# A trunk's mixer: PE's order left to the scheduler, or written out in groups of attention steps and projection chunks

## The chip, the cores and the metric

The kernel runs on one core of one Trainium2 chip. The metric is the device time of one execution in microseconds (us). The core has a matrix engine (TensorE, PE in the profile, with its weight loads as PEld), a vector engine (VectorE, DVE), a scalar engine (ScalarE, ACT), GpSimd (POOL) and SyncE (SP), which here only issues DMAs. Each engine runs its own queue of instructions in a fixed order and waits for the others through semaphores.

## The reference

Two layers over 256 tokens of width 1024. Each layer is a mixer and then a mixture of experts, each with a residual and a layer norm behind it. The mixer multiplies the tokens by one wide input projection and splits its columns among three causal token mixers and three gates:

```
nq, kc, vc, ks, vs, kw, vw, ng, dq, dk, dv, cq, ckv, kr, mg = split_cols(h @ w_in, IN_SPLITS)
o_nsa = nsa_mixer(...)      # 8 heads: compressed, selected and window attention, gated
o_diff = diff_mixer(...)    # 4 heads: softmax(q1 k1) - lam * softmax(q2 k2), then rms norm
o_mla = mla_mixer(...)      # 8 heads: latent attention, up-projections of cq and ckv, rope
g = sigmoid(mg).reshape(B, S, 3, D_MODEL)
y = g[:, :, 0] * (o_nsa @ w_br_nsa) + g[:, :, 1] * (o_diff @ w_br_diff) + g[:, :, 2] * (o_mla @ w_br_mla)
return y @ w_out
```

The experts are 16 SwiGLU networks with a routing that keeps two experts per token. Weights and data are float32.

## The kernel before

**Projections in chunks.** Every projection is cut into chunks that stand in a list `fq`. `F(n)` (L394) takes `n` of them. A chunk first splits its weights into a high and a low half (`split`, L365: a cast on ScalarE, L369, and a subtraction on VectorE, L370; two pairs of buffers), one chunk ahead of its use, then runs three matmuls per piece of 128 rows (`mm3`, L373, the lines L374 to L376), then empties its accumulator (`pa`, two PSUM buffers). `add_fm` (L408) makes feature-major chunks: 24 matmuls of 256 columns for q, kv, dq, dk and the gates, twelve for a branch projection. `add_tm` (L437) makes token-major ones, which fill both accumulators. Weights come through a ring of buffers on SP's queue (`Stream`, L80); a buffer is given back by `ST.done`, and `ST.add(ring, ...)` hands further buffers to the experts' weights once the attention no longer holds them.

**Attention in steps.** `cmp1` to `cmp6` (L505 to L613) build the compressed keys and values and their softmax. `cmp1` swaps the two groups' halves with small matmuls (L513); `cmp2(k0)` (L524) runs eight matmuls of one weight buffer (L533, 32 columns of weights each), and its last call also turns the hidden layer and starts its activation. `nsa_A(n)` (L667) computes the scores of two heads (`scores`, L629, matmuls at L624, one PSUM pair of buffers), their row maxima on VectorE (L639, L641) and the exponentials on ScalarE (`expo`, L646); `nsa_B(n)` (L678) scales them (L650) and transposes them (`transp`, L654, L627, two PSUM buffers `pT`, copied out by VectorE at L658); `nsa_C(i)` (L691) multiplies with the values. `diff_A` to `diff_D` (L729 to L770) and `mla_Z`, `mla_A`, `mla_B`, `mla_C` (L841 to L874) do the same for the other two mixers; `mla_Z` makes the transposed queries and keys of two heads through two `pT` buffers (copied at L849), `mla_n` and `mla_t` (L796, L806) normalise the latents and turn them, `mla_up` (L820) queues their up-projections, `mla_rope` (L833) is VectorE alone.

**Order.** The source writes attention steps and chunks in turn: `go(...)` (L1023) runs one step, then one chunk. But this order is only a priority. The program is built with `schedule_with_timeline_sim=True` (L1784): the framework lays the instructions of each engine in an order of its own, taking what its estimate says is ready; only data dependences and edges made by `tc.issue_after(ins)` bind it. Such an edge keeps the instructions traced in its block, on the engine of `ins`, behind `ins` in issue order, with no wait for `ins` to finish. Within a step, `row` (L615) chains matmuls so. Between steps and chunks nothing is chained.

Of the kernel before, what the change touches and what calls it, by code (L numbers as in the profile page):

```python
# [68 lines left out]
def trunk(ctx, tc, x, consts, pcol, rowv, gb, wfm, wng, wdv, wmla, wcmp, wcmp2, wu, wbr, wout, rw, mw1, mw3, mw2, out):  # L69
    import numpy as np  # L70
    nc = tc.nc
    slopes = [float(v) for v in _slopes(np)]
    V, A, T, G = nc.vector, nc.scalar, nc.tensor, nc.gpsimd

    cst = ctx.enter_context(tc.tile_pool(name="cst", bufs=1))
    hp = ctx.enter_context(tc.tile_pool(name="hp", bufs=1))
# [265 lines left out]
    def mixer(l, res, z, zf):  # L342
# [35 lines left out]
        fq = []  # L378
# [15 lines left out]
        def F(n=1):  # L394
            for _ in range(n):
                if not fq:
                    return
                c = fq.pop(0)
                c.ready()
                for d in fq:  # L400
                    d.ready()
                    if d.grp is None or d.grp != c.grp:
                        break
                for _ in c.mm(c.h):
                    pass
                c.post()
# [95 lines left out]
        X = {}  # L502
        xT = []

        def cmp1():  # L505
            cx, kvc = X["cx"], X["kvc"]
            XS = cx.tile([P, 2, 16, 2, 16], F32, name="XS", tag="x5")
            V.memset(XS[:, :, :, :, 15:16], 0.0)
            sw = pT.tile([P, 2, P], F32, name="pt")
            rows = [slice(64 * g, 64 * g + 64) for g in range(2)]  # L510
            for i in range(2):
                for g in range(2):
                    T.matmul(sw[rows[1 - g], i], ident[rows[g], rows[g]], kvc[rows[g], i, 1 - g], start=True, stop=True)  # L513
            for i in range(2):
                p0 = PC_POS + 32 * l + 16 * i
                for g in range(2):
                    for a in (g, 1 - g):
                        base = kvc[rows[a], i, a] if a == g else sw[rows[a], i]
                        src = bass.AP(tensor=base.tensor, offset=base.offset, ap=[list(base.ap[0]), [1, 16], [8, 15]])
                        V.tensor_tensor(out=XS[rows[a], i, :, g, 0:15], in0=src, op=ALU.add,  # L520
                                                           in1=pc[rows[a], p0:p0 + 16].unsqueeze(2).to_broadcast([64, 16, 15]))
            X["XS"] = XS

        def cmp2(k0):  # L524
            XS = X["XS"]
            if k0 == 0:
                X["hid"] = pO.tile([P, 256], F32, name="o")
            X["wc"] = ST.get((l, "c", k0 // 4)).rearrange("p (i k c) -> p i k c", i=2, k=4)
            hid, wc = X["hid"], X["wc"]
            for k in range(k0, k0 + 4):  # L530
                for i in range(2):
                    o = 64 * (k % 2) + 32 * i
                    T.matmul(hid[o:o + 32], XS[:, i, k].rearrange("p g c -> p (g c)"), wc[:, i, k % 4],  # L533
                             start=(k < 2), stop=(k > 13), skip_group_check=True)
            ST.done((l, "c", k0 // 4))
            if k0 < 12:
                return
            cx = X["cx"]
            hs = X["t1"][:, 512:768]
            A.copy(hs, hid)  # L540
            hid = pO.tile([64, 256], F32, name="o")
            T.matmul(hid, id2, hs, start=True, stop=True)
            hx = cx.tile([64, 3, 256], F32, name="hx", tag="x6")
            A.copy(hx[:, 0], hid)
            V.tensor_mul(hx[:, 1], hx[:, 0], hx[:, 0])
            V.tensor_scalar(hx[:, 1], hx[:, 1], 0.044715, 1.0, op0=ALU.mult, op1=ALU.add)
            V.tensor_mul(hx[:, 1], hx[:, 1], hx[:, 0])
            A.activation(hx[:, 2], hx[:, 1], AF.Tanh, scale=math.sqrt(2.0 / math.pi))
            V.tensor_scalar(hx[:, 2], hx[:, 2], 1.0, 0.5, op0=ALU.add, op1=ALU.mult)
            V.tensor_mul(hx[:, 2], hx[:, 2], hx[:, 0])  # L550
            X["hx"] = hx
# [54 lines left out]
        def cmp6():  # L606
            cp = X["cp"]
            cpp = pT.tile([P, 2, S], F32, name="pt")
            for t in range(2):
                for hf in range(2):  # L610
                    T.transpose(cpp[:, hf, t * P:(t + 1) * P],
                                cp[:, t, 4 * hf:4 * hf + 4].rearrange("p a c -> p (a c)"), ident)
            A.copy(cpT, cpp)  # L613
# [264 lines left out]
        def gates(b, j):  # L878
            def ev(m, ps):
                if j == 0 and m == 0:  # L880
                    gate[b] = (mh if b % 2 else mg).tile([P, KD, S], F32, name="gt", tag=f"gt{b % 2}")
                A.activation(gate[b][:, 4 * j + m], ps, AF.Tanh, scale=0.5)
            add_fm(f"g{b}{j}", xT, 4, ev)
# [63 lines left out]
        with tc.issue_after(X0["z", 1 if "yh" in X0 else 3]):  # L947
            i = A.copy(gl[:, 0], w[:, 0:4])
# [57 lines left out]
        cx = X["cx"] = M["ml"] = left.enter_context(tc.tile_pool(name="cx", bufs=1, reuse_waits="tile"))  # L1006
# [7 lines left out]
        G.tensor_add(id2, ident[:, 0:64], ident[:, 64:P])  # L1014
        kvc = X["kvc"] = X["t1"][:, 0:512].rearrange("p (i a j) -> p i a j", i=2, a=2)

        F(8)
        V.tensor_scalar(gts, gts, 1.0, 0.5, op0=ALU.add, op1=ALU.mult)
        add_fm("dq", xT, 4, lambda m, ps: A.copy(dqT[:, m], ps))
        add_fm("dk", xT, 4, lambda m, ps: A.copy(dkT[:, m], ps))  # L1020
        add_tm("dv", xT, 512, lambda t, ps: A.copy(dv[:, t], ps))

        def go(*items):  # L1023
            for it in items:
                it()
                F()

        def z(f, *a):
            return lambda: f(*a)

        cmp1()
        diff_prep()
        go(z(nsa_A, 0), z(cmp2, 0), z(nsa_A, 1), z(cmp2, 4), z(nsa_B, 0), z(cmp2, 8), z(nsa_B, 1), z(cmp2, 12))
        go(z(nsa_A, 2), cmp3, z(nsa_A, 3), cmp4)
        cmp5()
        F(2)
        cmp6()
        if l == 0:
            router_prep()
        mla_in()  # L1040
        gates(0, 0)
        gates(0, 1)
        go(z(nsa_C, 0), z(nsa_B, 2), z(nsa_A, 4), z(nsa_B, 3), z(nsa_A, 5), z(nsa_C, 1), z(nsa_B, 4), z(nsa_A, 6), z(nsa_B, 5),
           z(nsa_A, 7), z(nsa_C, 2), z(nsa_B, 6), mla_n, z(nsa_B, 7), z(diff_A, 0), z(nsa_C, 3), mla_t)
        ST.add(ring, [f"wt{NA}"])
        ST.pump()
        F(2)
        mla_up(0)
        gates(1, 0)
        branch(0)  # L1050
        gates(1, 1)
        go(z(diff_A, 1), z(diff_B, 0), z(diff_A, 2), z(diff_C, 0), z(diff_B, 1), mla_rope, z(diff_A, 3), z(diff_D, 0), z(diff_C, 1),
           z(mla_Z, 0), z(diff_B, 2), z(diff_D, 1), z(mla_A, 0), z(diff_C, 2), z(diff_B, 3), z(mla_Z, 1), z(diff_D, 2), z(mla_B, 0),
           z(diff_C, 3), z(mla_A, 1))
        ST.add(ring, [f"wt{NA + 1}", f"wt{NA + 2}"])
        ST.pump()
        F(len(fq))
        mla_up(1)
        F(2)
        branch(1)  # L1060
        gates(2, 0)
        gates(2, 1)
        go(z(diff_D, 3), mla_rope, z(mla_C, 0), z(mla_B, 1), z(mla_Z, 2), z(mla_A, 2), z(mla_C, 1), z(mla_Z, 3), z(mla_B, 2),
           z(mla_A, 3), z(mla_C, 2), z(mla_B, 3))
        F(1)
        mla_C(3)
        left.close()
        pS = scores_pool(2)
        rb = open_ring("rb", NB, RAW)
# [568 lines left out]
    with start as st:  # L1638
# [14 lines left out]
        z = raw_tiles(0)  # L1653
# [134 lines left out]
```

## Time and profile before

| | us |
|---|---|
| median of three runs | 1070.39 |
| lowest, highest | 1069.12, 1071.18 |
| the profiled execution | 1068.88 |
| its span, first to last instruction | 1067.2 |
| PE busy | 1032.4 (97%) |
| VectorE busy | 524.1 (49%) |
| ScalarE busy | 431.3 (40%) |

Busy times are unions of an engine's spans. Matmuls are pipelined and their ends are modelled, so the time of a stretch on PE is read from start to start. The first layer's mixer runs from about 20 to 303 us with its output projection and routing; its stretch with attention is 38 to 240 us, in the second layer 563 to 765 us.

### The profile page before, as it was taken

What the parts mean: (1) busy time and instruction counts of PE and PEld (TensorE: products, weight loads), DVE (VectorE), ACT (ScalarE), POOL (GpSimd) and SP (SyncE); (2) the same over time, 40 slices, a digit from 0 to 9 for tenths busy, and PEclk for the clock granted to TensorE, in tenths of its full rate; (3) what the DMA queues carried; (4) which work ended last, traced back from release to release, by engine and by line L of the source; (5) the groups of instructions that cost most, each with busy time, mean ns of one, the idle gap of its engine ahead of it and who ended that gap; (6) DMA issues with size and microseconds to landing.
All of it is one profiled execution on the core that took longest, in us unless ns stands there. A gap on an engine that the chain in (4) does not pass through costs nothing. (4 is left out here: it accounts for less than half of the span.)

```text
span 1067.2 us, 16963 instructions
## 1 busy us (share of the span) xinstructions
PE 1032.4 (97%) x6578; PEld 716.0 (67%) x6578; DVE 524.1 (49%) x1481; ACT 431.3 (40%) x1001; POOL 38.1 (4%) x58
## 2 busy tenths in 40 slices
PE   8999999999989999999999999999999999999995
PEld 7888988999854444444497888799998344434332
DVE  7746778776752111211295467877677220212014
ACT  6563776555322121211266547755553121211111
POOL 0200000000000001000001001000000000000001
PEclk8999999999999999999999999999999999999998
DMA  9664334539879999999455534344587999999951
GB/s 360 249 223 149 119 124 173 197 124 376 317 280 341 422 421 419 419 421 411 167 211 202 189 141 159 132 166 158 217 342 296 330 392 421 421 419 419 420 226 39
DMA packets 45402, 293.88 MB, mean 275 GB/s; under 512 B 5120, under 2 KB 7936, under 8 KB 11776
## 3 DMA queue, kind: packets, MB, share of 16 engines
q1 hardware_dynamic: 43008, 277.88, 67.2%
q0 software_dynamic: 1728, 12.58, 2.9%
q10 hardware_dynamic: 576, 2.24, 0.6%
q8 instruction: 54, 0.88, 0.3%
q14 instruction: 36, 0.29, 0.1%
HBM read 291.63 MB, written 1.05 MB: 274 GB/s over the span
## 5 line engine op out<-in xcount | busy, mean ns | idle before, releaser
L1549 PE MATMUL pt<-wt,xe 128*64 128x512 f32 x1024 | 236.6, 596 | 1.6 <-PEq L1447 1.4
L370 DVE TENSOR_TENSOR wlo<-wt,whi 128x1024 fp32r<-128x1024 f32 (+4 forms) x146 | 167.2, 1148 | 80.5 <-ACT whi L369 74.3
L369 ACT CAST whi<-wt 128x1024 fp32r<-128x1024 f32 (+4 forms) x146 | 143.6, 988 | 144.6 <-PE acc L375 105.8
L374 PE MATMUL acc<-hi,whi 128*128 128x256 f32 x576 | 165.3, 288 | 1.7 <-ACT whi L369 0.8
L376 PE MATMUL acc<-hi,wlo 128*128 128x256 f32 x576 | 163.9, 286 | 0.8 <-DVE wlo L370 0.8
L1549 PEld LDWEIGHTS pt<-wt,xe 128*64 128x64 f32 x1024 | 73.7, 137 | 132.3 <-issue 125.6
L375 PE MATMUL acc<-lo,whi 128*128 128x256 f32 x576 | 162.3, 282 | 0.0
L1594 PE MATMUL pt<-wt,gT 128*64 128x512 f32 (+1 forms) x544 | 114.8, 571 | 2.7 <-ACT gT L1580 2.7
L374 PEld LDWEIGHTS acc<-hi,whi 128*128 128x128 f32 x576 | 108.1, 188 | 7.8 <-issue 3.9
L376 PEld LDWEIGHTS acc<-hi,wlo 128*128 128x128 f32 x576 | 108.3, 188 | 4.2 <-DVE wlo L370 2.1
L375 PEld LDWEIGHTS acc<-lo,whi 128*128 128x128 f32 x576 | 108.7, 189 | 0.0
L1594 PEld LDWEIGHTS pt<-wt,gT 128*64 128x64 f32 x544 | 37.1, 137 | 67.9 <-issue 59.0
L1603 DVE TENSOR_TENSOR yl<-pt,yh 128x512 fp32r<-128x512 f32 (+1 forms) x34 | 22.2, 657 | 112.0 <-ACT yh L1602 112.0
L1602 ACT CAST yh<-pt 128x512 fp32r<-128x512 f32 (+1 forms) x34 | 18.9, 560 | 104.6 <-PE pt L1594 104.6
L374 PE MATMUL acc<-ob,whi 128*128 128x256 f32 x192 | 56.8, 296 | 1.1 <-DVE gt L891 0.8
L1570 DVE SCALAR_TENSOR_TENSOR g<-g,wsl,pt 128x512 f32<-128x512 f32 x16 | 12.0, 747 | 93.1 <-PE pt L1549 93.1
L375 PE MATMUL acc<-ob,whi 128*128 128x256 f32 x192 | 54.2, 282 | 0.0
L376 PE MATMUL acc<-ob,wlo 128*128 128x256 f32 x192 | 54.2, 284 | 0.0
L1575 ACT CAST CT<-pt 128x256 fp32r<-128x256 f32 x16 | 6.0, 372 | 107.2 <-PE pt L1573 107.2
L658 DVE COPY ts<-pt 128x384 f32<-128x384 f32 x56 | 30.5, 551 | 30.7 <-PE pt L627 30.6
L1569 DVE SCALAR_TENSOR_TENSOR g<-g,pt 128x512 f32<-128x512 f32 x16 | 11.0, 686 | 67.3 <-ACT g L1568 67.3
L1568 ACT ACTIVATE g<-pt 128x512 f32<-128x512 f32 x16 | 9.6, 597 | 84.1 <-PE pt L1549 84.1
(403 smaller groups left out, 1819.1 us busy)
## 6 DMA issues: line engine op xcount, KB each, us to landing
wt<-in_mw SPq DMA_DIRECT2D x178, 1024.0 KB, 12.2
wt<-in_wfm SPq DMA_DIRECT2D x38, 1024.0 KB, 4.8
wt<-in_wbr SPq DMA_DIRECT2D x12, 1024.0 KB, 4.8
wt<-in_mw POOLq DMA_DIRECT2D x12, 1024.0 KB, 14.5
wt<-in_wcmp SPq DMA_DIRECT2D x8, 1024.0 KB, 6.6
wt<-in_wout SPq DMA_DIRECT2D x8, 1024.0 KB, 8.2
wt<-in_wdv SPq DMA_DIRECT2D x4, 1024.0 KB, 6.2
wt<-in_wmla SPq DMA_DIRECT2D x4, 832.0 KB, 5.5
```

What stands on the lines that cost most here:

```text
L369: X["hi"] = A.copy(hi, src).ins
L370: X["lo"] = V.tensor_sub(lo, src, hi.bitcast(F32)).ins
L374: T.matmul(ps, a[0], b[0], start=start, stop=False)
L375: T.matmul(ps, a[0], b[1], start=False, stop=False)
L376: return T.matmul(ps, a[1], b[0], start=False, stop=stop)
L658: X["ts"] = V.tensor_copy(ts, pt).ins
L1549: i = T.matmul(hh[64 * j:64 * j + 64], xe[p][:, 2 * h + k, j * CAP:(j + 1) * CAP], wt[:, c0:c0 + FF], start=(h == 0 and k == 0), stop=(h = ...
L1569: V.scalar_tensor_tensor(g, g, 1.0, h1, op0=ALU.add, op1=ALU.mult)
L1570: V.scalar_tensor_tensor(g, g, wsl[:, p:p + 1], h3, op0=ALU.mult, op1=ALU.mult)
L1594: T.matmul(v[64 * j:64 * j + 64], gT[:, 2 * h + f, 64 * j:64 * j + 64], w2t[:, c0 + ks[0] * P:c0 + ks[1] * P], start=(h == 0 and f == 0), ...
L1602: X0["yh"] = A.copy(yh[:, d], v).ins
L1603: V.tensor_sub(yl[:, d], v, yh[:, d].bitcast(F32))
```

## The change

TensorE's interface is wrapped (`Pe`) so that the last matmul or transpose traced is known, and `block(f, ...)` traces `f` with an edge behind it. Attention steps are now put in groups; after each group two or three chunks are run. Each step is a block and the chunks of a group are one block, so PE gets them in the written order. `cmp1` moves up between the second and the third chunk of kv; the end of `cmp2` becomes a block of its own (`cmp2s`); `mla_n`, `mla_rope` and the queueing of gates and branches stand between the groups; the first `ST.add` comes a group earlier.

```
+    class Pe:
+        last = None
+        def matmul(self, *a, **kw):
+            i = nc.tensor.matmul(*a, **kw)
+            self.last = i.ins
+            return i
...
+    T = Pe()
+    def block(f, *a):
+        with tc.issue_after(T.last):
+            return f(*a)
...
-            if k0 < 12:
-                return
-            cx = X["cx"]
+
+        def cmp2s():
+            cx, hid = X["cx"], X["hid"]
             hs = X["t1"][:, 512:768]
...
-        F(8)
+        F(2)
+        block(cmp1)
+        block(F, 6)
         V.tensor_scalar(gts, gts, 1.0, 0.5, op0=ALU.add, op1=ALU.mult)
         add_fm("dq", xT, 4, lambda m, ps: A.copy(dqT[:, m], ps))
         add_fm("dk", xT, 4, lambda m, ps: A.copy(dkT[:, m], ps))
         add_tm("dv", xT, 512, lambda t, ps: A.copy(dv[:, t], ps))
-        def go(*items):
+        def go(n, *items):
             for it in items:
-                it()
-                F()
-        def z(f, *a):
-            return lambda: f(*a)
-        cmp1()
+                block(*it) if isinstance(it, tuple) else block(it)
+            block(F, n)
         diff_prep()
-        go(z(nsa_A, 0), z(cmp2, 0), z(nsa_A, 1), z(cmp2, 4), z(nsa_B, 0), z(cmp2, 8), z(nsa_B, 1), z(cmp2, 12))
-        go(z(nsa_A, 2), cmp3, z(nsa_A, 3), cmp4)
-        cmp5()
-        F(2)
-        cmp6()
-        if l == 0:
-            router_prep()
+        go(2, (nsa_A, 0), (cmp2, 0), (cmp2, 4))
+        go(3, (nsa_A, 1), (nsa_B, 0), (cmp2, 8), (cmp2, 12))
+        go(2, (nsa_A, 2), (nsa_B, 1), cmp2s)
+        go(2, (nsa_A, 3), cmp3)
+        go(2, cmp4)
         mla_in()
         gates(0, 0)
         gates(0, 1)
-        go(z(nsa_C, 0), z(nsa_B, 2), z(nsa_A, 4), z(nsa_B, 3), z(nsa_A, 5), z(nsa_C, 1), z(nsa_B, 4), z(nsa_A, 6), z(nsa_B, 5),
-           z(nsa_A, 7), z(nsa_C, 2), z(nsa_B, 6), mla_n, z(nsa_B, 7), z(diff_A, 0), z(nsa_C, 3), mla_t)
+        go(3, cmp5)
+        if l == 0:
+            router_prep()
+        go(2, cmp6)
+        go(2, (nsa_C, 0), (nsa_B, 2), (nsa_A, 4))
+        mla_n()
+        go(2, (nsa_B, 3), (nsa_A, 5))
+        go(2, (nsa_C, 1), (nsa_B, 4), (nsa_A, 6))
+        gates(1, 0)
+        go(2, (nsa_B, 5), (nsa_A, 7))
         ST.add(ring, [f"wt{NA}"])
         ST.pump()
-        F(2)
+        go(2, (nsa_C, 2), (nsa_B, 6), (diff_A, 0), mla_t)
         mla_up(0)
-        gates(1, 0)
         branch(0)
         gates(1, 1)
-        go(z(diff_A, 1), z(diff_B, 0), z(diff_A, 2), z(diff_C, 0), z(diff_B, 1), mla_rope, z(diff_A, 3), z(diff_D, 0), z(diff_C, 1),
-           z(mla_Z, 0), z(diff_B, 2), z(diff_D, 1), z(mla_A, 0), z(diff_C, 2), z(diff_B, 3), z(mla_Z, 1), z(diff_D, 2), z(mla_B, 0),
-           z(diff_C, 3), z(mla_A, 1))
+        go(2, (nsa_B, 7), (diff_A, 1))
+        go(2, (nsa_C, 3), (diff_B, 0))
+        go(2, (diff_C, 0), (diff_B, 1), (diff_A, 2))
+        mla_rope()
+        go(2, (diff_D, 0), (diff_B, 2), (diff_A, 3), (mla_Z, 0))
+        go(3, (diff_C, 1), (diff_C, 2), (diff_B, 3), (mla_A, 0))
+        go(3, (diff_D, 1), (diff_D, 2), (diff_C, 3), (mla_Z, 1), (mla_B, 0))
         ST.add(ring, [f"wt{NA + 1}", f"wt{NA + 2}"])
         ST.pump()
-        F(len(fq))
+        go(len(fq), (diff_D, 3), (mla_A, 1))
         mla_up(1)
-        F(2)
+        block(F, 2)
         branch(1)
         gates(2, 0)
         gates(2, 1)
-        go(z(diff_D, 3), mla_rope, z(mla_C, 0), z(mla_B, 1), z(mla_Z, 2), z(mla_A, 2), z(mla_C, 1), z(mla_Z, 3), z(mla_B, 2),
-           z(mla_A, 3), z(mla_C, 2), z(mla_B, 3))
-        F(1)
-        mla_C(3)
+        mla_rope()
+        go(2, (mla_C, 0), (mla_B, 1), (mla_Z, 2))
+        go(2, (mla_C, 1), (mla_A, 2))
+        go(2, (mla_Z, 3), (mla_B, 2))
+        go(2, (mla_C, 2), (mla_A, 3))
+        go(3, (mla_B, 3))
+        block(mla_C, 3)
         left.close()
         pS = scores_pool(2)
         rb = open_ring("rb", NB, RAW)
```

## Rows read from the trace of the kernel before

**Rows 1.** Page, first part: busy us (share of the span) xinstructions.
```profile
PE 1032.4 (97%) x6578; PEld 716.0 (67%) x6578; DVE 524.1 (49%) x1481; ACT 431.3 (40%) x1001; POOL 38.1 (4%) x58
```
**Rows 2.** Busy time by stretch: layer 0's mixer with attention; its experts.
```profile
38.00:240.00 202.00, 199.99 (x1529) 175.75 (x1529) 142.91 (x439) 125.00 (x335) 11.08 (x15) 1.00 0.46 162
...
303.00:528.00 225.00, 220.33 (x1111) 96.35 (x1109) 38.96 (x97) 38.38 (x79) 3.71 (x8) 1.00 0.94 378
```
**Rows 3.** Page, costliest groups: busy, mean ns, idle before and its releasers.
```profile
L1549 PE MATMUL pt<-wt,xe 128*64 128x512 f32 x1024 | 236.6, 596 | 1.6 <-PEq L1447 1.4
```
**Rows 4.** Groups of PE, 38 to 240.3 us (layer 0), then 563 to 765 us.
```profile
L624 PE MATMUL s<-hold 64*128 64x128 f32 (+1 forms) x96 | 13.2, 354 | 0.0
L533 PE MATMUL o<-wt,XS 128*32 128x256 f32 x64 | 6.9, 388 | 0.0
...
L624 PE MATMUL s<-hold 64*128 64x128 f32 (+1 forms) x96 | 14.7, 358 | 0.0
L533 PE MATMUL o<-wt,XS 128*32 128x256 f32 x64 | 7.3, 388 | 0.0
```
**Rows 5.** Timeline of PE, one score block: start us, us, line, tiles.
```profile
40.65 0.49 PE L624 MATMUL s<-hold 64*128 64x128 f32 x2
41.06 0.40 PE L375 MATMUL acc<-wlo,hi 128*128 128x280 f32 x1
41.30 0.29 PE L376 MATMUL acc<-whi,lo 128*128 128x280 f32 x1
...
41.90 0.92 PE L624 MATMUL s<-hold 64*128 64x128 f32 x6
```
**Rows 6.** Timeline of PE, another score block.
```profile
134.53 0.93 PE L624 MATMUL s<-hold 64*128 64x128 f32 x8
135.38 0.39 PE L374 MATMUL acc<-hi,whi 128*128 128x256 f32 x1
```
**Rows 7.** Timeline of PE, transposes and the chunk behind them.
```profile
143.51 0.82 PE L627 MATMUL pt<-idb,e 128*128 128x128 f32 x6
144.08 0.36 PE L374 MATMUL acc<-hi,whi 128*128 128x256 f32 x1
144.28 0.28 PE L375 MATMUL acc<-lo,whi 128*128 128x256 f32 x1
```
**Rows 8.** Timeline of PE, compression: 22 records in one piece.
```profile
45.25 1.07 PE L533 MATMUL o<-wt,XS 128*32 128x256 f32 x16
...
46.14 0.61 PE L533 MATMUL o<-wt,XS 128*32 128x256 f32 x6
```
**Rows 9.** Timeline of PE, a pause of the projection stream.
```profile
162.31 0.28 PE L375 MATMUL acc<-lo,whi 128*128 128x256 f32 x1
163.38 0.38 PE L374 MATMUL acc<-hi,whi 128*128 128x256 f32 x1 [0.80 <-ACT whi L369]
```
**Rows 10.** Timelines of VectorE and ScalarE behind one MLA score block.
```profile
222.19 0.28 DVE L639 CUSTOM_DVE_ANT_0 e<-s,CA 128x128 f32<-128x128 f32 x1
...
222.51 0.41 ACT L647 ACTIVATE e<-e,mn 128x128 f32<-128x128 f32 x1 [2.14 <-DVE mn L639]
...
224.44 1.05 ACT L369 CAST whi<-wt 128x1024 fp32r<-128x1024 f32 x1
...
226.40 0.50 ACT L652 ACTIVATE e<-e,r 128x256 f32<-128x256 f32 x1
```
**Rows 11.** Timeline of PE: first matmul of a branch chunk, and what follows it.
```profile
180.83 0.36 PE L374 MATMUL acc<-ob,whi 128*128 128x256 f32 x1
...
182.34 0.27 PE L627 MATMUL pt<-idb,e 128*128 128x128 f32 x1
```
**Rows 12.** Timelines of ScalarE and VectorE: a transposed latent is taken out.
```profile
149.12 0.47 ACT L815 ACTIVATE cTh<-pt,pc 128x256 fp32r<-128x256 f32 x1 [1.31 <-PE pt L813]
...
149.98 0.48 DVE L816 SCALAR_TENSOR_TENSOR cTl<-pt,pc,cTh 128x256 fp32r<-128x256 f32 x1
```
**Rows 13.** Busy time by stretch: up-projections and differential attention, layer 0.
```profile
155.00:192.00 37.00, 35.11 (x274) 32.23 (x273) 31.63 (x126) 26.14 (x80) 0.00 (x0) 1.00 0.46 160
```

More of the change, by code (lines that the diff above doesn't have):

```diff
@@ L72, in trunk, with transpose @@
     slopes = [float(v) for v in _slopes(np)]
-    V, A, T, G = nc.vector, nc.scalar, nc.tensor, nc.gpsimd
+    V, A, G = nc.vector, nc.scalar, nc.gpsimd
+    class Pe:
[4 more added lines that the diff above has]
+            return i
+        def transpose(self, *a):
+            i = nc.tensor.transpose(*a)
+            self.last = i.ins
+            return i
+    T = Pe()
+    def block(f, *a):
+        with tc.issue_after(T.last):
+            return f(*a)
     cst = ctx.enter_context(tc.tile_pool(name="cst", bufs=1))
```

## The prediction

> **What bounds the kernel now.** I read the page first: TensorE (PE) is busy 97% of the span [rows 1]. A busy PE is not a PE at its peak, so the next view is busy time by stretch: in the first layer's mixer PE is busy 199.99 of 202 us while VectorE has 142.91 and ScalarE 125.00, the weights' DMA share is 0.46, and the granted clock is 1.00, the 2.4 GHz level [rows 2]. In the experts' stretch the DMA share is 0.94 [rows 2], yet the experts' up matmuls waited 1.6 us in total over 1024 records, none of it named as a landing [rows 3]. So the time is the sum of the steps from one PE start to the next, in both stages, and what the change takes from the mixer's PE stream shifts all that follows. It touches the mixer only, twice (layers 0 and 1).
>
> What is to be had there is seen in the timeline of PE. The projection stream starts a 256-column matmul every 0.12 us. The list of groups in the two mixer windows shows what its interruptions cost: the 64 compression records are busy 6.9 and 7.3 us, the 96 score records (twelve score blocks of eight) 13.2 and 14.7 us [rows 4]. Compare a score block that runs in two pieces, 0.41 us for its first two records and then 0.92 for the rest, with projection matmuls between [rows 5], with a whole one, 0.93 busy and 0.85 us from start to next start [rows 6]. A block that is broken pays its tail twice. Transposes are different: six of them, 143.51 to 144.08, then a projection matmul with 0.20 instead of 0.12; the last transpose hands over after 0.03 instead of 0.11, so going between transposes and projections costs nothing [rows 7]. So it isn't the number of interruptions that costs, but the number of pieces of scores, compression and attention-output matmuls.
>
> **What the change takes away.** Before, PE's order comes from the scheduler, which puts in whatever is ready; after, each block is queued behind the last PE instruction of the block before, so no block is broken. PE meets some 26 stints of attention per layer.
> Compression: sixteen records in a row take 0.89 us (45.25 to 46.14) [rows 8]. After, they stand as 32 and 32: 4 x 0.89 and two tails, 3.9 us, against 6.9 and 7.3 [rows 4]: 3.0 + 3.4 = 6.4 us. Seven pieces fewer per layer also spare the slow first matmul after each (the nearest row is that after a score piece, 41.06 to 41.30, 0.24 where 0.13 is usual [rows 5]), some 0.1 x 14: 1.5. Together 8 us.
> Scores: twelve whole blocks at 0.93 are 11.2 us, against 13.2 and 14.7 [rows 4, 6]: 2.0 + 3.5 = 5.5, and about ten returns at 0.15: 7 us.
> The head swap of the compression, the compressed scores (three pieces before) and an MLA output that was broken: no more than 1.5 us in all; taken as 1.5, bound below by 0.
> Pauses: in layer 0 five starts of the stream come late, the worst at 162.31, whose successor starts 1.07 us later, with 0.80 idle until ScalarE's cast [rows 9]; from their sizes I make it 2.6 us in layer 0 and 1.9 in layer 1, 4.5 together. They stand where up-projection, rope and differential attention meet on ScalarE and VectorE. The groups space these out, so I take them as gone; bounds 0 and 4.5.
> Sum: 8 + 7 + 1.5 + 4.5 = 21 us; with the low bounds 15.
>
> **What it adds.** No instruction is new; `cmp2s` is the tail of `cmp2`, and the slot of the ring is handed out a group earlier, which moves one expert load forward on a queue that has room [rows 2]. What is new is order: PE now waits at the head of a block, and everything behind it, the projection chunks too, waits with it. Where there was always a chunk to fill in, there is now a distance fixed by hand. So each group is tested by the time from producer to consumer against PE's work between.
> The length of the chain: scores to exponentials, sums, scaling, transposes. In [rows 10] VectorE begins at 222.19, the exponentials at 222.51, a cast of the weights (1.05 us) pushes in at 224.44, scaling ends at 226.90. So 4.7 us with the cast and 3.7 without; with some 0.3 us from the last score to VectorE's start, 4 to 5 us to the second half, and 0.7 less to the first.
> PE's work between: a chunk of the branch projection is only twelve matmuls, 1.5 us (180.83 to 182.34) [rows 11], half of a gate chunk. Two of those are 3 us, less than the chain.
> Per layer, then: (a) the last MLA block (`mla_A` 3, two branch chunks, `mla_B` 3): 0.4 at the first half, 0.4 at the second: 0.8, up to 2 with a cast in the way. (b) `mla_Z` 3 and `mla_B` 2 in one group need four transposition buffers where there are two; a buffer is freed by VectorE's copy: 0.7. (c) the same in the group with `diff_D` 1 and 2, `mla_Z` 1, `mla_B` 0: 1.0. (d) `mla_t` behind `nsa_B` 6 and `diff_A` 0: three transpositions through two buffers, the third waits for ScalarE's 0.47 and for VectorE's 0.48, which stood behind four score reductions (149.12 to 150.46) [rows 12]: 1.4. (e) `mla_Z` 2 comes right after `mla_up`'s chunks, with `mla_rope` on VectorE between, and the next split is late behind it: 1.5. (f) `diff_B` 2 and 3: 4.5 to 5 us of distance for a chain of 4 to 6: 0.8. (g) up-projection chunks back to back, whose two accumulators must first be emptied: 0.8. (h) compressed softmax before `cmp6`, and short chunks whose split has only one chunk to hide behind: 0.5.
> Sum 7.5 per layer, 15 us. The nsa groups themselves add nothing: two gate chunks and a stint lie between every step and its consumer, 9 us and more against a chain of 5. Bounds: without any cast in the way and with the buffers freed at once 3 per layer; with a cast or a split (1.05, 1.2) in front at each place 11 per layer.
> The Trainium skill, "PSUM — Partial Sum Buffer", section "Engine vs sequencer instructions", has it that matmuls start and complete in program order; this speaks against the change, since nothing passes a block that waits. By that rule the 15 us are paid in full, and without it they would be near 0 and the time near 1049; the trace agrees with it where it can show it, as PE sat idle 0.80 us at 163.38 [rows 9].
>
> **Sum.** 21 - 15 = 6 us less. The profiled execution took 1068.88 us around a span of 1067.2; the median of the three runs is 1070.39, 1.5 higher. Taken from the median: 1064.4, say **1064 us**.
>
> **Rivals.** (1) Slower: VectorE becomes the bound in the differential groups. In 155 to 192 us it is busy 31.63 of 37 us, 85% [rows 13], and PE's pauses stand there. Before, PE could take a chunk when VectorE was behind; after, a late copy, a late reciprocal root or a late split stops PE, and the stop delays VectorE's next input in turn. If each such group stretches by a tenth, that is 3.7 us per layer beyond (c) and (f), so 11 to 12 per layer: 23 - 21 = +2 and more, some 1073 us. It decides from 10.5 us of new waits per layer. Against it: VectorE's work is unchanged, and PE's own stretch gets only a few per cent shorter. (2) The distances hold: new waits at their lower bound, 6 us for both layers: 21 - 6 = 15 less, 1055 us. For it speaks that the groups leave two splits' worth of room at almost every place, so the cast need not be in the way. (3) No change: the experts' weights, not PE, end the stage. DMA runs at 0.94 there [rows 2]; a mixer that ends earlier would only make PE wait for weights, 1070 us. Against it: no record of a wait for a landing [rows 3], and the loads start when the mixer frees their buffers, so they move with it.
>
> **How the numbers follow.** Forecast (1059 to 1068): 0.52. Rival 2: 0.18. Rival 1: 0.16. Rival 3: 0.14. About 0.2% (2.1 us) is what a measurement of this kernel can tell from no change. Faster: 0.52 + 0.18 = 0.70. Same: 0.14 and the edge of rival 1, 0.15. Slower: 0.15. The range reaches from rival 2 with its best (21 - 5 = 16 less, 1054) to 1071, just beyond no change; it leaves out most of rival 1. The forecast's own range is 1059 to 1068.
>
> **What would show it.** Compression busy about 3.9 us and scores about 11.2 us per mixer window in the list of groups; no score block in two pieces in PE's timeline. Waits of PE on VectorE's and ScalarE's results (`ts`, `qk`, `cTl`, scaled `e`), which are all but absent now, 15 us of them, at the places (a) to (h), most in the last third of each mixer. The experts' stretches should keep their length. I am wrong if the mixer shrinks by over 7 us a layer (waits overestimated), if PE's waits exceed 10 us a layer, or if PE waits for landings in the experts' stretch.

## The result: 2.5% slower, and where the 27 us come from

The changed kernel takes 1096.6 us (median; 1095.8 to 1097.7) against 1070.2 us for the kernel before: a ratio of 1.025, 95% interval 1.023 to 1.0265. Forecast were 1064 us, with a chance of 0.15 that it would be slower, so the prediction is wrong in sign. Between the profiled spans (1067.2 and 1094.9 us) lie 27.7 us, and these are accounted for below.

First, which stretch grew. Below is busy time by stretch of the kernel after (the stretch, its length, then busy us of PE, PEld, VectorE, ScalarE and GpSimd, then the granted clock, the share of DMA and GB/s): the two mixers from their first projection to the first matmul of the output projection, and between them the experts of layer 0.

```profile
27.87:273.75 245.88, 232.28 (x1785) 208.36 (x1783) 166.13 (x467) 143.00 (x363) 12.85 (x19) 0.98 0.49 180
315.00:540.00 225.00, 220.14 (x1104) 96.71 (x1106) 40.00 (x100) 38.59 (x79) 3.71 (x8) 1.00 0.94 379
564.58:809.50 244.92, 231.09 (x1783) 207.37 (x1782) 163.87 (x462) 142.94 (x363) 11.56 (x13) 0.99 0.49 176
```

The same stretches of the kernel before:

```profile
27.79:260.63 232.84, 230.83 (x1784) 206.35 (x1783) 162.55 (x467) 141.22 (x363) 13.34 (x19) 1.00 0.52 190
551.11:785.23 234.12, 232.71 (x1784) 207.09 (x1783) 161.92 (x462) 142.18 (x364) 13.10 (x13) 1.00 0.51 184
```

The mixers are 13.0 and 10.8 us longer. PE is busy nearly as long as before (232.28 against 230.83) but stands still for 13.6 and 13.8 us in place of 2.0 and 1.4, and the clock is no longer 1.00. In the experts' row PE's busy time is that of before [rows 2] to 0.2 us. The rest of the span's 27.7 us, some 3.4, comes in layer 1's routing (below).

What PE now waits for, over the whole span (engine, line waited for, total us, times, longest):

```profile
PE pt L84 <- ACT ot L781: 11.0, 5, 3.0
PE pt L84 <- ACT e L669: 3.8, 4, 1.4
PE pt L84 <- DVE qm L798: 3.6, 2, 1.8
...
PE pt L84 <- DVE cTl L834: 2.4, 2, 1.2
...
PE pt L79 <- DVE mxf L1422: 1.8, 1, 1.8
...
PE acc L79 <- ACT whi L387: 1.6, 2, 0.8
```

All of PE's matmuls now have line 79 and its transposes line 84, since they go through the wrapper. Transposes of `ot` are those of the differential output (`diff_D`): they wait for `diff_C`'s scaled result. That is the largest wait. It is at none of the places (a) to (h) of the prediction; only rival 1 names a late reciprocal root, without a place.

What was to be taken away did go. The groups of scores and compression in layer 0, then in layer 1, against [rows 4]:

```profile
L79 PE MATMUL s<-hold 64*128 64x128 f32 (+1 forms) x96 | 11.8, 368 | 0.0
L79 PE MATMUL o<-wt,XS 128*32 128x256 f32 x64 | 3.9, 382 | 0.0
...
L79 PE MATMUL s<-hold 64*128 64x128 f32 (+1 forms) x96 | 11.1, 350 | 0.0
L79 PE MATMUL o<-wt,XS 128*32 128x256 f32 x64 | 3.9, 382 | 0.0
```

Compression is at the 3.9 us that was forecast; the scores are at 11.1 where the clock was full, forecast 11.2.

Now the whole account of both mixers, made from PE's timeline from each start to the next, with the idle time before a record taken out, and what ran at the 1.2 GHz level counted at half its length:

| both mixers, us | forecast | measured |
|---|---|---|
| compression, its records | -6.4 | -5.6 |
| scores, their records | -5.5 | -4.8 |
| first matmuls after a piece (steps of the projections) | -3.0 | -5.6 |
| small pieces | -1.5 | -0.6 |
| pauses of before | -4.5 | -3.4 |
| idle of PE after | +15 | +27.4 |
| longer steps of transposes | 0 | +7.4 |
| stretches at 1.2 GHz | not in the sum | +8.5 |

That makes +23.3; with 0.5 in other steps it is the mixers' 23.8, and the routing's 3.4 and 0.5 elsewhere make the span's 27.7.

Two of these rows need care. Where a transpose hands over to a projection matmul, the transpose's step is 0.04 us and the projection's 0.22; without the hand-over they are 0.12 and 0.13. Both mixers of before have 55 such hand-overs, those of the kernel after 20, so some 2.6 us are taken off the projections' row and put on the transposes', and are neither won nor lost. Without them the takings are some 17.4 us of 20.9 forecast, and the new waits, idle time and longer transposes together, some 32 us in place of 15. So the sum failed on its second half, and a term, the clock, is missing.

**The largest wait, step by step.** PE of the kernel after, layer 0, from `diff_C` 0 to its transposes:

```profile
165.43 0.83 PE L79 MATMUL o<-hold,ts 128*128 128x128 f32 x6
...
171.66 0.28 PE L79 MATMUL acc<-ob,wlo 128*128 128x256 f32 x1
174.91 0.69 PE L84 MATMUL pt<-idb,ot 128*128 128x128 f32 x2 [2.97 <-ACT ot L781]
```

And what stands between them on ScalarE and VectorE (from two timelines, in order of time):

```profile
165.51 1.05 ACT L387 CAST whi<-wt 128x1024 fp32r<-128x1024 f32 x1 [2.16 <-PE acc L79]
...
167.10 1.22 DVE L388 TENSOR_TENSOR wlo<-wt,whi 128x1024 fp32r<-128x1024 f32 x1
168.23 0.16 DVE L778 TENSOR_SCALAR ss<-ss 128x2 f32<-128x2 f32 x1
168.30 0.28 DVE L657 CUSTOM_DVE_ANT_0 e<-s,alibi 128x128 f32<-128x128 f32 x1
...
169.41 0.17 DVE L240 TENSOR_SCALAR rqy<-ss 128x2 int32<-128x2 int32 x1
...
171.84 1.23 DVE L388 TENSOR_TENSOR wlo<-wt,whi 128x1024 fp32r<-128x1024 f32 x1 [0.42 <-ACT whi L387]
...
174.04 0.15 DVE L246 SCALAR_TENSOR_TENSOR rqy<-rqt,rqy 128x2 f32<-128x2 f32 x1
174.23 0.63 ACT L781 ACTIVATE ot<-o,rqy 128x128 f32<-128x128 f32 x2 [1.46 <-DVE rqy L246]
```

The chain is: a cast in front of the squares, a split in front of the mean (`ss`), four score reductions (168.30 to 169.41), three rounds of the reciprocal root, 0.2 us for each little step, a second split and three more large operations in front of the last step at 174.04. From the end of `diff_C` (166.26) to the scaled output (174.86) it is 8.6 us; the change had put 5.5 us of PE's work there (166.26 to 171.8). The chain binds PE only, so what slips in on VectorE is still what the scheduler chose.

The same distance stood in the trace of before, in rows that the prediction never read, PE twice and ScalarE once:

```profile
156.44 0.83 PE L624 MATMUL o<-hold,ts 128*128 128x128 f32 x6
...
168.04 0.62 ACT L763 ACTIVATE ot<-o,rqy 128x128 f32<-128x128 f32 x2 [0.82 <-DVE rqy L228]
...
169.55 0.38 PE L627 MATMUL pt<-idb,ot 128*128 128x128 f32 x2
```

Before, that result took 11.4 us from the end of `diff_C` and PE came for it after 12.3. Over all eight of them in both layers the result took 8.0 to 11.8 us, and PE came after 11.6 to 17.8. A written order that leaves 5.5 us had to wait for it, though in the kernel after the four results that PE waits some 3 us for come a little sooner (8.3 to 9.4 us behind `diff_C`).

**The clock.** Behind that wait PE runs at half rate. The kernel after, in stretches of 2 us:

```profile
174.00:176.00 2.00, 1.09 (x5) 0.93 (x5) 0.20 (x2) 0.99 (x3) 0.00 (x0) 0.63 0.89 266
176.00:178.00 2.00, 2.00 (x12) 1.17 (x11) 0.97 (x3) 0.11 (x1) 0.00 (x0) 0.50 0.65 266
178.00:180.00 2.00, 2.00 (x11) 1.91 (x10) 2.00 (x10) 1.69 (x8) 0.00 (x0) 0.50 0.61 106
180.00:182.00 2.00, 2.00 (x14) 2.00 (x14) 1.39 (x5) 1.15 (x5) 0.00 (x0) 0.66 0.98 414
```

A granted clock of 0.50 is the 1.2 GHz level. There are four such stretches in the two mixers (174.5 to 181.3, 242.8 to 246.2, 727.5 to 730.9, 778.7 to 782.1 us), and none in the mixers of before. Two begin within the waits of 2.97 and 2.76 us that end at 174.91 and 727.59; the other two begin 1.8 and 1.9 us after waits of 1.38 us have ended. Half their length, some 8.5 us, is lost. The Trainium skill, "TensorE: Matmul & The Clock Gate", section "HAM oscillation — how this bites in real kernels", describes this: a wait between bursts of matmuls lets the array fall back to 1.2 GHz, so that the next burst starts slow. The trace agrees with it at the first stretch (0.50 behind 2.97 us of idle).

### The profile page after: what moved, and what is told of

Its sections match the earlier page's. It is cut to its first block, busy times and chain, and to the rows that moved or that the text cites. A ratio compares the mean times of both kernels' runs of the same rounds, so it can differ in the third digit from the quotient of the medians.

```text
span 1094.9 us, 16968 instructions
## 1 busy us (share of the span) xinstructions
PE 1034.5 (94%) x6578; PEld 718.7 (66%) x6578; DVE 529.9 (48%) x1481; ACT 434.3 (40%) x1001; POOL 36.1 (3%) x58
## 5 line engine op out<-in xcount | busy, mean ns | idle before, releaser
L79 PE MATMUL acc<-ob,whi 128*128 128x256 f32 x384 | 73.4, 291 | 0.8 <-DVE gt L909 0.8
L79 PEld LDWEIGHTS acc<-ob,whi 128*128 128x128 f32 x384 | 60.8, 193 | 2.0 <-DVE gt L909 1.2
L665 ACT ACTIVATE e<-e,mn 128x128 f32<-128x128 f32 x64 | 25.3, 396 | 39.5 <-DVE mn L657 39.5
```

Source lines behind the costliest of these rows:

```text
L79: i = nc.tensor.matmul(*a, **kw)
L665: A.activation(e[:, 0:128], e[:, 0:128], AF.Exp, bias=mn[:, 0:1], scale=-1.0, accum_out=sums[0])
```

## The experiments

Theory A: it is the chain. PE stands at the head of a block whose data are not there, with chunks behind it that could run. Rival B: it is the written order itself, chained or not. Rival C: VectorE is simply full there. Two more questions are about the clock and about the removal.

| | us | ratio to before, 95% interval | mixers of layers 0 and 1, us |
|---|---|---|---|
| before | 1070.2 | | 232.8, 234.1 |
| after | 1096.6 | 1.023 to 1.0265 | 245.9, 244.9 |
| no chain | 1072.9 | 1.001 to 1.0034 | 233.1, 234.2 |
| chain up to the seventh score block | 1056.7 | 0.985 to 0.988 | 226.8, 226.7 |
| chain from there on | 1101.7 | 1.0275 to 1.031 | 249.8, 248.8 |
| steps chained, chunks free | 1058.5 | 0.987 to 0.991 | 227.7, 227.4 |
| steps chained, chunks free from there on | 1061.2 | 0.990 to 0.993 | 228.4, 228.4 |
| old order, chained | 1115.4 | 1.040 to 1.0465 | 255.1, 256.0 |
| three chunks moved up | 1083.6 | 1.0095 to 1.015 | 242.2, 240.0 |
| no wait for the root | 1086.4 | 1.013 to 1.017 | 242.7, 239.8 |
| waits filled | 1085.5 | 1.012 to 1.015 | 243.4, 241.5 |
| waits filled, one place more | 1094.1 | 1.021 to 1.0265 | 242.3, 242.0 |
| before, compression grouped | 1066.1 | 0.996 to 0.998 | 230.9, 230.6 |

The last column is from PE's timeline, from the mixer's first projection matmul to the first one of the output projection.

### The chain taken off

```diff
     def block(f, *a):
-        with tc.issue_after(T.last):
-            return f(*a)
+        return f(*a)
```

> The order stays as written, but no block is queued behind the one before it: the scheduler may again put a projection chunk wherever a block is not ready. Theory A (the chain costs: PE stands at the head of a block whose data are not there): nearly all of PE's new waits in the mixers (26.8 us of idle in both against 3.3 before) go, and with them the stretches at the 1.2 GHz level; some blocks break again. Some 1060 to 1074 us. Rival B (the written order costs: consumers stand too close behind producers and load VectorE and ScalarE at the wrong time, chained or not): 1085 us or more, with waits on VectorE and ScalarE of over 15 us.

1072.9 us, at the upper end of A's range. PE's idle in the mixers is back at 2.3 and 2.5 us, with the order otherwise as written. Rival B falls: the order alone costs next to nothing. It gains nothing either. Compression is broken again, 5.3 us in each layer, and, against A, the low clock is not gone: one stretch is left in each mixer (166.8 to 170.3 and 692.5 to 695.9 us), behind waits of 0.99 and 0.98 us for a cast. The first, from PE's timeline and from the busy times by stretch:

```profile
166.74 1.16 PE L79 MATMUL acc<-whi,cTh 128*128 128x512 f32 x2 [0.99 <-ACT whi L386]
...
168.00:170.00 2.00, 2.00 (x6) 1.26 (x6) 0.95 (x9) 0.77 (x2) 0.00 (x0) 0.50 0.62 158
```

Half of the two, 3.4 us, is lost; without it this order would have gained some 1.5 us per mixer on the kernel before.

### The chain kept where nothing waited

```diff
-        with tc.issue_after(T.last):
+        with tc.issue_after(T.last) if T.on else nullcontext():
...
+        T.on = False
         go(2, (nsa_C, 2), (nsa_B, 6), (diff_A, 0), mla_t)
```

> The chain holds up to the seventh score block of the compressed-attention part (where PE showed no wait) and ends there; differential and MLA groups keep their written order but may be mixed with chunks. Theory A: compression stays at 3.7 us and most score blocks whole, the waits in the last third go: 1056 to 1066 us, below both kernels. Rival B (order, not chain): 1085 us or more.

Chained are the groups up to `nsa_A` 7, free those from `nsa_C` 2 on. 1056.7 us, within A's range, and faster than both kernels. The groups of layer 0's mixer:

```profile
L79 PE MATMUL s<-hold 64*128 64x128 f32 (+1 forms) x96 | 11.8, 351 | 0.0
L79 PE MATMUL o<-wt,XS 128*32 128x256 f32 x64 | 3.9, 382 | 0.0
```

Both mixers by stretch:

```profile
27.81:254.64 226.83, 225.57 (x1785) 205.04 (x1783) 163.63 (x467) 141.77 (x363) 12.55 (x19) 1.00 0.54 195
...
546.31:773.05 226.74, 225.53 (x1783) 204.84 (x1782) 161.64 (x462) 142.25 (x364) 12.14 (x13) 1.00 0.53 190
```

Compression stays whole, idle is 1.3 and 1.2 us, the clock is 1.00, and each mixer is 6.0 and 7.4 us shorter than before. So the chain is worth its removal where data are always there, and costs where they are not.

### The chain only where PE waited

Against the kernel of the last experiment:

```diff
-        T.on = True
+        T.on = False
         F(2)
         block(cmp1)
...
-        T.on = False
+        T.on = True
         go(2, (nsa_C, 2), (nsa_B, 6), (diff_A, 0), mla_t)
```

> The reverse of the kernel chained in its first part only: everything up to the seventh score block is free, and the chain begins at the third group's output step of compressed attention and holds to the end of the mixer. Theory A (the gain belongs to the first part of the chain, the loss to the second, and they add up): the loss is that from the kernel chained in the first part to the one chained throughout, 1096.6 - 1056.7 = 39.9 us, on top of the free kernel's 1072.9: 1108 to 1115 us. Rival: the first part's chain brings the second its waits, by bunching; then 1090 us or less.

1101.7 us: slower than the changed kernel, as A has it, but below A's range and 11 us short of its sum. The two halves do not add up: the first part's chain is worth 13.8 us in the mixers where the second part is free (no chain against chain up to there) and 7.7 us where it is chained. Of the 13.8, 3.4 are the low clock of the kernel with no chain, which the kernel chained up to there does not have in its mixers; where the second part is chained, both have it alike (some 8 us). The cause of the rest stays open. The waits are those of the changed kernel: 10.7 us in 4 for `ot`.

### Chunks free, steps chained

```diff
             for it in items:
                 block(*it) if isinstance(it, tuple) else block(it)
-            block(F, n)
+            F(n)
```

> The changed kernel, with the attention steps chained to one another as before, but the projection chunks handed out without a chain, so that they may fill a wait (and break a block). Theory A: it is that no chunk may pass that costs; idle of PE in the mixers under 8 us, 1058 to 1072 us. Rival B (the order of the attention steps costs by itself): 1083 us or more.

1058.5 us, in A's range: the attention steps may be bound to each other in the written order, if chunks may pass. Idle is 2.5 us per mixer, the score blocks stay whole. A variant of both, chunks chained up to the seventh score block and free behind it:

```diff
-        with tc.issue_after(T.last) if T.on else nullcontext():
+        with tc.issue_after(T.last) if T.on or f.__name__ != "F" else nullcontext():
```

> All attention steps chained to one another throughout, the projection chunks chained as far as the seventh score block (as with the chain up to there alone), free behind it. If whole blocks are worth what the kernel before suggests, the score blocks of the last third come whole too (10.3 us in place of 11.0 per mixer) and no new wait comes in: 1054 to 1057 us. Rival: steps that wait for one another hold up later steps, and what is won in whole blocks goes into waits, as where all chunks were free: 1057 to 1060 us.

A miss, 1061.2 us: above even its rival's range. In each mixer it is 0.7 to 0.9 us behind the kernel with free chunks, not ahead: idle 3.2 us in place of 2.5. Layer 1's routing is 1.6 us longer, with the same late start of an expert's matmul as in the kernel after, and layer 0's is 1.1 us shorter.

### The old order, chained

```diff
             for it in items:
-                it()
-                F()
+                block(it)
+                block(F)
```

> The order of the kernel before as it was written (one chunk after each step, compression in four parts), with every step and every chunk of it queued behind the last PE instruction of the one ahead. Theory A (the chain makes the waits, whichever order is chained): over 15 us of new idle on PE in the mixers, stretches at the 1.2 GHz level, 1080 to 1100 us. Rival B (it is the new order): no more than 5 us of new idle, 1064 to 1075 us.

(`cmp5`, `cmp6` and the chunks that stand outside `go` have no edge of their own, but the blocks behind them are chained to them.) 1115.4 us, slower by more than A said. PE's waits:

```profile
PE pt L84 <- ACT ot L781: 14.0, 4, 3.7
PE pt L84 <- DVE cp L621: 13.1, 2, 6.6
```

Two chains make 27 us: the differential output again, and the compressed softmax (`cmp5` to `cmp6`, 6.6 us each), for which the new order has found room. So the new order is the better one to chain; it is only not good enough.

### The root out of the chain

```diff
             for t in range(2):
-                A.activation(ot[:, t], o[:, t], AF.Copy, scale=rs[:, t:t + 1])
+                A.activation(ot[:, t], o[:, t], AF.Copy, scale=0.1)
```

> The changed kernel, but the output of a differential block is scaled by a constant in place of its reciprocal root, so that the result of the root is computed on VectorE as before and waited for by nobody; the output is another one. Theory A1 (the chain of small VectorE steps between the differential output and its transposes, 8.9 us long against 5.9 us of PE work, is what PE waits for): the wait of 11.0 us in 5 pieces falls under 3, the 1.2 GHz stretches behind it go: 1081 to 1088 us. Rival C (VectorE is simply full there; whatever it does last is waited for): the waits move to the transposes of the scaled weights and to the queries' copies; 1092 us or more.

1086.4 us, inside A1's range, but only part of A1 holds. The wait for `ot` is gone; in its place stand two that the kernel after hadn't:

```profile
PE pt L84 <- ACT e L669: 3.8, 4, 1.4
PE pt L84 <- DVE qm L798: 3.6, 2, 1.8
PE pt L84 <- DVE e L763: 3.1, 4, 1.4
PE pt L84 <- DVE ob L507: 3.1, 2, 1.6
```

The first two rows are those of the kernel after. The last two (6.2 us) are new: the weighted difference of `diff_B` and the split of `diff_D`'s output, next in VectorE's queue. Of 11.0 us, 6.2 come back, as C has it. The mixers gain 8.3 us, clock included: layer 1's is at 1.00 throughout, layer 0's still falls twice (191.2 and 239.0 us).

### Distance instead

```diff
-        go(2, (diff_C, 0), (diff_B, 1), (diff_A, 2))
+        go(3, (diff_C, 0), (diff_B, 1), (diff_A, 2))
...
-        go(3, (diff_C, 1), (diff_C, 2), (diff_B, 3), (mla_A, 0))
+        go(5, (diff_C, 1), (diff_C, 2), (diff_B, 3), (mla_A, 0))
```

> The changed kernel, chain and all, with the three chunks that stood in the last differential group moved up: one more (1.5 us) between differential output 0 and its transposes, two more (some 5.9 us, gate chunks) between outputs 1, 2 and theirs. Theory A1 (a distance that is too short by the wait's own length): of the two waits of some 3 us per layer the first falls to about 1.5 and the second goes, and one or two 1.2 GHz stretches per layer with them: 1084 to 1089 us. Rival C (VectorE full): each chunk brings a 1.2 us split, the chain of small steps gets longer by as much, 1094 us or more.

1083.6 us. Outputs 0, then 1 and 2 of layer 0, PE's timeline:

```profile
165.06 0.83 PE L79 MATMUL o<-hold,ts 128*128 128x128 f32 x6
...
175.03 0.44 PE L84 MATMUL pt<-idb,ot 128*128 128x128 f32 x2 [1.54 <-ACT ot L781]
...
180.38 1.50 PE L79 MATMUL o<-hold,ts 128*128 128x128 f32 x12
...
192.18 0.60 PE L84 MATMUL pt<-idb,ot 128*128 128x128 f32 x4
```

As A1 said: one more chunk halves the first wait (2.97 to 1.54), two more end the second. One of 1.6 to 1.9 us per layer, for the split of the output (`ob`, L507), is new. The result of output 0 comes 0.5 us later than without the chunk (9.1 us after `diff_C`'s end), which is C's part: a third of the 1.5 us. The clock did less than A1 said: of the four low stretches three are left in the profiled execution, at 197.0, 238.0 and 729.5 us. No computing was left out here, so this is the cleanest evidence that the distance was too short.

### Waits filled with matmuls that nobody needs

```diff
+        def fill(pt, n):
+            return [mm(pt[:, 0:256], xT[k % 8][0][:, 0:P], xT[k % 8][0], start=True, stop=True) for k in range(n)]
...
-            row(*[tr(otp[:, t * P:(t + 1) * P], ot[:, t], ident) for t in (1, 0)])
+            row(*fill(otp, (20, 0, 20, 0)[hd]), *[tr(otp[:, t * P:(t + 1) * P], ot[:, t], ident) for t in (1, 0)])
```

and likewise 12 ahead of the first half of `mla_B` 3.

> The changed kernel with matmuls that compute nothing wanted put ahead of three kinds of transposes that PE waits for: 20 (2.4 us) each before those of differential outputs 0 and 2, 12 (1.4 us) before those of the last MLA block. Theory D (the low clock after a wait is a cost of its own, some 8.6 us in the two mixers): the waits are filled rather than shortened, the granted clock stays at 1.00 through both mixers, and the kernel gets faster by 4 to 9 us although PE does 12 us more work: 1088 to 1093 us. Rival E (the low level has nothing to do with PE's being idle): the clock falls at the same places and the time is 1097 us or more.

1085.5 us: 11 us faster with some 13 us more work on PE (104 matmuls), more than forecast; 5.9 of it lies in the mixers, which is what D speaks of. The same 2 us stretches as above:

```profile
174.00:176.00 2.00, 1.43 (x15) 1.05 (x13) 0.50 (x2) 1.10 (x3) 0.00 (x0) 1.00 0.82 295
176.00:178.00 2.00, 2.00 (x19) 1.75 (x16) 1.98 (x11) 1.19 (x6) 0.00 (x0) 1.00 0.90 258
178.00:180.00 2.00, 2.00 (x19) 2.00 (x18) 1.64 (x6) 1.99 (x7) 0.00 (x0) 1.00 0.90 377
```

The data are no earlier: the transposes of output 0 start at 174.70 against 174.91. But what follows, the same list of instructions up to `diff_C` 1, takes 5.35 us (174.70 to 180.05) in place of 8.27 (174.91 to 183.18). That is D: the low level is a price of its own, on top of the wait, and it follows PE's standing still. Of the four low stretches none is left; one came up at 217.2 to 220.6 us, behind the wait of 1.8 us for `mla_Z` 2, which was not filled. In the mixers the gain is 2.5 and 3.4 us. D's sum for that is 5.1 us of low clock less 1.7 for the new stretch in layer 0, and 3.4 in layer 1; in part it is offset by filling too long (output 2 lay ready at 188.03, its transposes begin at 190.56). The spans differ by 9.6 us; 3.3 of it lies in layer 1's routing, where this kernel's expert matmul starts on time and the clock stays at 1.00, and nothing of the edit is there.

One place more, ahead of the transposes of `mla_Z` 2:

```diff
-                row(*[tr(tq[:, n, t * P:(t + 1) * P], v[:, t, hh], ident) for t in (1, 0) for n, v in ((0, qm), (1, km))])
+                row(*fill(tq[0:96].rearrange("p a s -> p (a s)"), 16 if c == 2 and j == 0 else 0),
+                    *[tr(tq[:, n, t * P:(t + 1) * P], v[:, t, hh], ident) for t in (1, 0) for n, v in ((0, qm), (1, km))])
```

> As with the filling matmuls at three kinds of places, and 16 more (1.9 us) ahead of the transposes of the third MLA block's queries, where the first mixer's granted clock still fell after a wait of 1.8 us. Theory D (the low level follows PE's standing still): that last stretch at 1.2 GHz goes, 2 to 3 us: 1081 to 1084 us. Rival E: no change, 1085 to 1088 us.

A miss in time, 1094.1 us, though both mixers now show no granted clock under 1.00. Layer 0's mixer is 1.1 us shorter, not 2 to 3, layer 1's 0.5 longer. What is lost lies in layer 1's routing, 1.5 us, and in layer 0's experts, 5.2 us:

```profile
431.81 1.45 PE L79 MATMUL pt<-wt,xe 128*64 128x512 f32 x5
436.20 1.60 PE L79 MATMUL pt<-wt,xe 128*64 128x512 f32 x4 [2.94 <-issue]
```

That is a pause of 2.9 us at an expert's matmul for which the profile names no cause, with DMA at a share of 1.01 and a granted clock of 0.83 in the 10 us around it. A late landing of weights would be the prediction's third rival in small; but the last weights before it landed at 434.79, 1.4 us before the matmul starts, so the cause stays open.

### One part of the change, in the kernel before

```diff
-        go(z(nsa_A, 0), z(cmp2, 0), z(nsa_A, 1), z(cmp2, 4), z(nsa_B, 0), z(cmp2, 8), z(nsa_B, 1), z(cmp2, 12))
+        go(z(nsa_A, 0), z(nsa_A, 1), two(0), z(nsa_B, 0), z(nsa_B, 1), two(8))
```

where `two(k)` runs `cmp2(k)`, `cmp2(k + 4)` and a chunk, each behind the last.

> The kernel before with one part of the change alone: the four compression steps stand in two pairs, each pair and the chunk behind it chained, the rest mixed by the scheduler. If the price of broken compression was read rightly: its records take 3.7 us per mixer in place of 6.9 and 7.3, with the first matmuls after the pieces 6 to 8 us in all: 1062 to 1065 us. Rival (what is saved there is lost in what the scheduler now breaks instead): 1067 to 1071 us.

1066.1 us, 0.2 to 0.4% faster than before and 1 us above the range. Compression takes 3.9 us in each mixer, as expected, but the mixers gain only 1.9 and 3.6 us: the end of the second pair now waits 1.3 us per mixer for ScalarE's copy of the hidden layer. And layer 1's routing got 2.8 us longer. So the removal is real, and half of it is easily lost.

## Why the prediction was wrong, point by point

**What bounds the kernel** was read rightly: PE's steps in the mixers. The experts' stretches kept their length (from the first up matmul to the last 213.5 us in layer 0 in both kernels, 213.5 and 215.3 in layer 1, where 1.7 us are a stretch at 1.2 GHz at its start), so the third rival did not come.

**What is taken away** was right in the main: 20.9 us forecast, some 17.4 measured without the hand-overs that only change rows. The first matmuls after a piece then come out at the 3.0 forecast; the scores, the compression, the small pieces and the pauses are each 0.7 to 1.1 us short.

**"Transposes cost nothing"** [rows 7] is true of going between them and projections, before and after alike, and was no help here: in the kernel after 23 transposes stand in front of a wait, in the kernel before one. Each is put down as some 0.29 us long in place of 0.11, and the wait is counted only from there, so that some 4 us of waiting stand in the view of busy time and not in that of waits.

**What it adds** is the step that failed. Per layer, forecast first: (d) `mla_t`, 1.4 forecast, 1.4 measured (145.61, idle 1.22). (e) `mla_Z` 2: 1.5 and 1.8 to 2.0. (c) the group with `mla_Z` 1 and `mla_B` 0: 1.0 and 0.9 without the wait for `ot`. (a) the last MLA block: 0.8 and 2.1, its upper bound. (b) 0.7 and 1.0. (g) up-projection: 0.8 and 2.0; the wait that the profile shows there is for a cast (`whi`, 0.8), not for the accumulators. (h) 0.5 and 1.5. (f) 0.8: hidden behind the wait for `ot`. Together some 11 us per layer, which is the upper bound. And the place that is missing altogether, `diff_C` to `diff_D`: 5.5 us idle per layer. The prediction tested every group by one chain, scores to weights, 4 to 5 us. The differential mixer has a second, longer one, and the list was made without it.

**The point where rival 1 decides** (10.5 us per layer) was passed, and rival 1 had the mechanism in part: the differential groups, late on VectorE, in-order behind splits and reductions. Its price (1073) was 24 us too low, and its picture, that VectorE is full, holds for about half: with the root taken out, 6.2 of 11.0 us came back, but with more distance the wait ends and VectorE does the same work. In the chain shown above VectorE even stands idle for 0.42 us, since the split at 171.84, in front of the root's last steps, waits for its cast.

**Program order.** The Trainium skill, "PSUM — Partial Sum Buffer", section "Engine vs sequencer instructions", on matmuls in program order, was cited as speaking against the change, and the runs bear it out: with the chain off, PE's idle is 2.3 and 2.5 us per mixer, with it 13.6 and 13.8.

**The missing term** is the clock. It is 8.5 us in the mixers and some 1.7 in the routing. The kernel before has no row that shows it in the mixers; but a sum that adds 15 us of waits to PE owed a sentence on it, and an upper bound.

**Layer 1's routing**, 3.4 us longer, was not foreseen. PE's first expert matmul, after and then before:

```profile
853.70 3.63 PE L79 MATMUL pt<-wt,xe 128*64 128x512 f32 x8 [1.79 <-DVE mxf L1422]
...
827.77 1.94 PE L1549 MATMUL pt<-wt,xe 128*64 128x512 f32 x8 [0.15 <-DVE xe L1381]
```

The first expert's matmul starts 1.8 us late, and the clock is at 1.2 GHz behind it (1.7 us more). The reduction named there (`mxf`) runs on VectorE in the same place of its order as before and is no operand of the matmul. Yet the matmul starts 0.06 us behind its end, here and in four more kernels of the study (no chain; steps chained, chunks free from there on; waits filled, one place more; before, compression grouped), and 0.06 us behind the end of the first `xe`, its operand, in the kernel before and the seven others. A landing of weights isn't it: the one nearest ahead came at 852.93, its like in the kernel before came 0.87 us after the matmul's start. Why the built program waits for `mxf` in some kernels and not in others stays open.

## What to carry to other kernels

A hand order that PE cannot leave pays where each consumer's data are there in any case, and costs where they are not; so chain the part of the program where the trace of the free order shows PE coming late to every result, and leave the rest to fill in. Before writing such an order, read for each pair of producer and consumer how long the result really took in the trace (8.0 to 11.8 us here) and not how long its operations are, because other work stands in front of them on the other engines. And where a change makes PE wait, price the wait twice: its own length, and the matmuls behind it at the lower clock.

## What was not expected of the hardware

The clock fell behind some waits and not behind others of the same size: behind 2.97 us idle at 174.91 and 1.38 at 240.98, but not behind 2.37 at 193.21 or 2.69 at 711.31. With no chain it fell behind 0.99 us, where the mixer as a whole stood still for 2.3 us only. Length alone does not say which. Nor are the falls the same in every execution of one kernel: with three chunks moved up the four executions took 1081.65, 1082.24, 1084.98 and 1085.52 us at mean granted clocks of 0.995, 0.993, 0.988 and 0.990, and the profiled one is that at 0.988. And the clock falls in the routing, where PE's work is thin: the kernel before had the 2.4 GHz level throughout its routing, while the kernel chained in its first part shows

```profile
290.00:294.00 4.00, 3.90 (x15) 3.90 (x16) 3.72 (x25) 2.20 (x5) 0.00 (x0) 0.57 0.51 168
```

in a stretch of the program that no experiment touched; its routing is 1.2 us longer for that in each layer. Differences of 1 to 3 us between two kernels of this study can come from there alone.
